# Channels 4 to 11 of a hybrid gMLP and attention step in pairs by seven half-length products, and gate sums in strips on the tensor engine

## The chip, the cores and the metric

The kernel runs on one core of a Trainium2 chip. The core has TensorE (PE in the profile, with its weight loads as PEld), VectorE (DVE), ScalarE (ACT), GpSimd (POOL) and SyncE (SP), which here issues the DMAs. Each engine has a queue of its own and works it off in order; engines wait for each other by semaphores. The metric is the device time of one execution in microseconds. Before the change the median of three runs is 626.75 us (626.26 to 626.86).

## The reference, cut to what matters

One step of a trunk with 128 context tokens and 1024 latent tokens, 1152 in all. The input is normalised, modulated and multiplied with one wide projection. Its columns are u, v and a gate g_a (512 each), the parts of the attention (c_q, c_kv, k_rope, together 448) and a gate g_b (512).

```python
def _front(x, cond, norm_g, w_ada, b_ada, w_in, w_s, b_s, g_v, q_norm_g, w_uq, kv_norm_g):
    mod = jax.nn.silu(cond) @ w_ada + b_ada
    shift, scale, gate = jnp.split(mod[:, None, :], 3, axis=-1)
    h = _rmsnorm(x, norm_g) * (1 + scale) + shift
    u, v, g_a, c_q, c_kv, k_rope, g_b = _split_in(h @ w_in)
    a_out = _chunk_mlp(u, v, w_s, b_s, g_v) * jax.nn.silu(g_a)
    ...

def _chunk_mlp(u, v, w_s, b_s, g_v):
    u = jax.nn.gelu(u)
    v = _rmsnorm(jax.nn.gelu(v).reshape(B, L, A_HEADS, A_HEAD_DIM), g_v)
    mixed = jnp.einsum('hpq,bnqhd->bnphd', w_s, v) + b_s.T[:, :, None]
    return u * mixed.reshape(B, L, A_WIDTH)

def _back(x, gate, a_out, attn, g_b, w_o):
    y = jnp.concatenate([a_out, attn * jax.nn.silu(g_b)], axis=-1) @ w_o
    return x + gate * y
```

## The kernel before

The transposed, modulated input h lies in SBUF as eight blocks of 128 features by three token groups of 384 tokens, each in two parts of a reduced format, a high part `hh[k, g]` and a low part `hl[k, g]` (the program's area0, area1 and area2 are the groups; a block's two parts stand side by side). A product of full precision takes three passes: high by high, high by low and low by high.

The twelve channel blocks of 128 columns are u (0 to 3, gelu), g_a (4 to 7, silu) and g_b (8 to 11, silu). For each block and group TensorE does 8 x 3 matmuls into one PSUM bank. For u and g_a, ScalarE writes the activation to SBUF and GpSimd multiplies it into `mixA`; for g_b ScalarE writes it into `mixB`. The weights of a channel come by one DMA of 512 KB (`w2r`) and are split into a high part (`w2h`, GpSimd) and a low part (`w2l`, VectorE).

The stages in order: modulation, transposes and the v projection; then a planned stretch (up to about 130 us) with the rest of v, channels 0 to 2 and the mixes `mixp` of the nine token tiles in four groups (0 to 2, 3 to 5, 6 and 7, 8); then channels 3 to 11 in a plain loop; then the z stage (`zacc`, from 245 us), attention and the output projection.

The planned stretch is written as steps with an engine, a cost, the steps they depend on and a priority. A planner replays them with these costs and records each engine's instructions in the order that comes out; this order is what the queues hold. The plain loop is recorded as it is written. There, beside the channels, `gate_sums` makes the third part of the modulation: VectorE multiplies each block of weights (`adag`) by a scalar per partition and adds it up (`matvec`, line 315), ScalarE and VectorE split the sums into two parts, and two matmuls with ones (line 830) add up the partitions. The weights of z (`wqr`, eight of 224 KB) are also split there, on GpSimd.

## Time and profile before

| What | Value |
|---|---|
| Median of three runs | 626.75 us |
| The profiled execution: its own time | 626.29 us |
| The profiled execution: span of its instructions | 624.5 us |
| GpSimd, ScalarE, VectorE busy | 29%, 42%, 58% of the span |
| Channels 3 to 11 on TensorE | 130.1 to 245.05 us |
| A w2r load of 512 KB, issue to landing, median | 3.9 us |

The span is what the trace covers; the rest of the execution's own time lies around it. Busy time of an engine is a sum over the whole span and says nothing of which engine is waited for; that is read from the chain of waits and from single stretches. Matmul records overlap, so their pace is the distance of their starts and not their duration.

### The profile page before, as it was taken

The page shows a single profiled execution, that of the slowest core. Times are in us where ns is not written, and L with a number is a line of the kernel's source. Part 1 is how long each engine was busy: PE and PEld are TensorE (multiplying, and loading weights), DVE is VectorE, ACT ScalarE, POOL GpSimd, SP SyncE. Part 2 cuts the span into 40 slices and gives each one's busy share as a digit, 9 for nine tenths or more (in the row PEclk, how much of TensorE's full clock was granted, in tenths as well). Part 3 has the DMA queues.
Part 4 walks back from the last instruction along what each step waited for, and adds up shares of the span by engine and source line. Part 5 has one row for each costly group of instructions (what it writes and reads, how often), then busy time and mean ns, then how long its engine had stood idle before and what let it go on. Part 6 is the DMA issues. An engine that isn't in the chain of part 4 may idle for free.

```text
span 624.5 us, 9810 instructions
## 1 busy us (share of the span) xinstructions
PE 610.4 (98%) x3703; PEld 555.3 (89%) x3703; DVE 364.4 (58%) x841; ACT 264.5 (42%) x636; POOL 178.8 (29%) x217
## 2 busy tenths in 40 slices
PE   7999999999999999999999999999999999999994
PEld 7678889999999999999997899999999988888884
DVE  4693466049556100476678657776666754587654
ACT  7556753112111111555676565555545632232212
POOL 2461223345545500443263212323222341000001
PEclk8999999999999999999999999999999999999998
DMA  8992000051331203000010000001101023423311
GB/s 319 391 373 69 1 34 2 2 180 71 116 108 58 94 8 110 27 2 1 1 41 1 2 0 2 1 2 35 35 1 34 35 69 129 142 101 135 128 41 68
DMA packets 15967, 46.32 MB, mean 74 GB/s; under 512 B 1952, under 2 KB 4912, under 8 KB 15920
## 3 DMA queue, kind: packets, MB, share of 16 engines
q1 hardware_dynamic: 15776, 45.51, 20.4%
q8 instruction: 29, 0.48, 0.3%
q10 hardware_dynamic: 144, 0.20, 0.1%
q14 instruction: 18, 0.15, 0.1%
...
## 4 chain that ended last, share of the span: by engine, by line
PE 92%; DVE 3%; ACT 2%; DMA 1%; issue 1%; SPq 0%; ACTq 0%; DVEq 0%
PE tp L746 6%; PE tp L159 6%; PE tp L157 6%; PE tp L158 6%; PE pT L1255 5%; PE w L1504 5%; PE w L1502 5%; PE w L1503 5%; PE o L1279 3%; PE o L1281 3%; PE o L1280 3%; PE s L1210 3%; PE s L1211 3%; PE s L1209 3%; PE s L1208 3%; PE s L1212 3%
## 5 line engine op out<-in xcount | busy, mean ns | idle before, releaser
L111 DVE TENSOR_TENSOR pl<-pT,ph 128x512 fp32r<-128x512 f32 x81 | 55.5, 687 | 48.4 <-ACT ph L1259 48.3
L1199 POOL TENSOR_SCALAR e<-e,rs 128x1280 f32<-128x1280 f32 x32 | 42.9, 1340 | 133.4 <-DVE rs L1198 121.1
L159 PE MATMUL tp<-area,w2l 128*128 128x384 f32 x216 | 72.5, 336 | 0.0
L157 PE MATMUL tp<-area,w2h 128*128 128x384 f32 x216 | 72.5, 336 | 0.0
L158 PE MATMUL tp<-area,w2h 128*128 128x384 f32 x216 | 72.5, 336 | 0.0
L1193 ACT ACTIVATE e<-s,nb,scl 128x256 f32<-128x256 f32 x64 | 56.1, 880 | 37.5 <-DVE nb L1187 37.5
L1259 ACT CAST ph<-pT 128x512 fp32r<-128x512 f32 x80 | 45.4, 588 | 42.0 <-PE pT L1255 39.0
L1255 PE MATMUL pT<-ident,e 128*128 128x128 f32 x320 | 48.0, 272 | 1.1 <-DVE pl L111 1.0
L1279 PE MATMUL o<-ph,vh 128*128 128x256 f32 x160 | 47.8, 299 | 0.0
L111 DVE TENSOR_TENSOR w2l<-w2r,w2h 128x1024 fp32r<-128x1024 f32 x12 | 19.9, 1655 | 45.7 <-POOL w2h L114 45.7
L1281 PE MATMUL o<-ph,vl 128*128 128x256 f32 x160 | 44.9, 281 | 0.0
L1280 PE MATMUL o<-pl,vh 128*128 128x256 f32 x160 | 44.7, 280 | 0.0
L1504 PE MATMUL w<-area,ml 128*128 128x512 f32 (+1 forms) x114 | 43.2, 379 | 0.0
L1255 PEld LDWEIGHTS pT<-ident,e 128*128 128x128 f32 x320 | 37.4, 140 | 4.6 <-issue 1.4
L157 PEld LDWEIGHTS tp<-area,w2h 128*128 128x128 f32 x216 | 40.5, 188 | 0.6 <-issue 0.5
L158 PEld LDWEIGHTS tp<-area,w2h 128*128 128x128 f32 x216 | 40.5, 188 | 0.2
L159 PEld LDWEIGHTS tp<-area,w2l 128*128 128x128 f32 x216 | 40.5, 188 | 0.0
L1208 PE MATMUL s<-kch,area 128*128 128x512 f32 (+2 forms) x100 | 39.2, 392 | 1.3 <-ACT e L1193 1.3
L1183 DVE TENSOR_REDUCE m<-s 128x1 f32<-128x1024 f32 x32 | 38.9, 1216 | 0.9 <-PE s L1212 0.8
L746 PE MATMUL tp<-area,w2h 128*128 128x384 f32 x144 | 37.3, 340 | 0.0
L1211 PE MATMUL s<-krh,area 128*128 128x512 f32 (+2 forms) x100 | 35.4, 354 | 0.0
L1210 PE MATMUL s<-kch,area 128*128 128x512 f32 (+2 forms) x100 | 35.4, 354 | 0.0
...
## 6 DMA issues: line engine op xcount, KB each, us to landing
...
```

The lines of the kernel that those rows point to most:

```text
L111: V.tensor_tensor(lo, src, f32(hi), op=ALU.subtract)
L157: T.matmul(ps, wh, xh, start=j == 0, stop=False)
L158: T.matmul(ps, wh, xl, start=False, stop=False)
L159: T.matmul(ps, wl, xh, start=False, stop=j == n - 1)
L746: T.matmul(tps[i, g][:, :GW], w_[i][:, k, :], x_[k, g], start=k == 0 and j == 0, stop=k == NK - 1 and j == 2)
L1193: S.activation(e[:, sl], src, AF.Exp, bias=nb, scale=scl[:, t : t + 1], accum_out=su[:, i : i + 1])
L1208: T.matmul(ps, qh_, kch[:, sl], start=True, stop=False)
L1255: T.transpose(ps[:, w : w + P], es[t, h][:, c * P : (c + 1) * P], ident)
L1279: T.matmul(o, vh[:, kt, :], ph[:, sl], start=c == 0, stop=False)
L1280: T.matmul(o, vh[:, kt, :], pl[:, sl], start=False, stop=False)
L1281: T.matmul(o, vl[:, kt, :], ph[:, sl], start=False, stop=c == n - 1)
L1504: T.matmul(ps, b, woh[k][:, c0:c1], start=False, stop=k == NK - 1)
```

## The change

Channels 0 to 3 are done as before, all in the planned stretch, which now goes on through all channels and the start of z. Channels 4 to 11 form four pairs (i, j). For token groups 0 and 1 the pair's 2 x 2 blocks (two channels by two halves of the features) times the input's 2 x 2 blocks (two halves by two groups) are done by seven products of half the length instead of eight, `p1` to `p7`: four use sums of input blocks (`t1` to `t4`), four use sums of weight blocks (`s1` to `s4`). The results are put together by additions from PSUM (`ka` to `kh`). Group 2 of these channels is done in the plain way.

The input sums are made once, by `input_sums`, on VectorE and GpSimd with ScalarE's casts; the first sum `t1` takes the place of `hh[k, 1]`, so `input_back` restores those blocks before z. The weight sums are made for each pair. High parts of weights from channel 2 on are made by ScalarE. The gate sums go to TensorE: eight matmuls into four strips of 32 partitions, then two matmuls with a selecting matrix; their load is one of 1 MB for each of four parts. The weights of z come in four loads, and their splits move to ScalarE, GpSimd and VectorE.

```diff
--- before.py
+++ after.py
@@ weights in parts @@
     def split_steps(i, deps):
         def hi():
-            a, b = ((0, 1), (2, 3), (6, 7))[i % 3]
-            w2hi[i] = slot(a, f"w2h{i}", [8, P], F32R)
-            w2lo[i] = slot(b, f"w2l{i}", [8, P], F32R)
-            pool_copy(w2hi[i], w2raw[i])
-        step(f"w2h{i}", "G", 1.01, hi, [f"w2r{i}", *deps], 2)
-        step(f"w2{i}", "V", 1.14, lambda: lo_of(w2lo[i], w2raw[i], w2hi[i]), [f"w2h{i}"], 3)
+            first = 6 if i == 2 else 8 if i == 3 else 2 * (i % 2)
+            w2hi[i], w2lo[i] = (weight_slot(first + m, f"w2{i}{m}", [8, P]) for m in range(2))
+            if i < 2:
+                pool_copy(w2hi[i], w2raw[i])
+            else:
+                S.copy(w2hi[i], w2raw[i])
+        step(f"w2h{i}", "G" if i < 2 else "S", 1.2, hi, [f"w2r{i}", *deps], 2)
+        step(f"w2{i}", "V", 1.4, lambda: lo_of(w2lo[i], w2raw[i], w2hi[i]), [f"w2h{i}"], 3)
@@ input sums, then undone @@
+    def input_sums(k, prio):
+        b11, b12, b21, b22 = ((f32(hh[kk, g]), f32(hl[kk, g])) for kk, g in ((k, 0), (k, 1), (k + 4, 0), (k + 4, 1)))
+        (h2, l2), (h3, l3) = T2[k], T3[k]
+        free = [f"v{t}" for t in range(5, 9)]
+        c = {}
+        ...
+        two("t1u", "G", made_in("u1", lambda: sub(G, c["u1"], b12[1], b11[1]), 2), ["sx", *older("t1s")])
+        two("t1a", "V", made_in("t1", lambda: sub(V, c["t1"], b12[0], b11[0])), ["sx"])
+        two("t1s", "V", lambda: add(V, c["t1"], c["t1"], c["u1"]), [f"t1u{k}", f"t1a{k}"])
+        two("t2a", "V", made_in("t2", lambda: sub(V, c["t2"], b22[0], c["t1"]), 2), [f"t1s{k}", *older("t2")])
+        two("t2s", "G", lambda: add(G, c["t2"], c["t2"], b22[1]), [f"t2a{k}"])
+        two("t2h", "S", lambda: S.copy(h2, c["t2"]), [f"t2s{k}", *free])
+        two("t3u", "G", made_in("u3", lambda: sub(G, c["u3"], b22[1], b12[1]), 3), [f"t3s{k - 1}"] if k else ["h27"], takes=("hf",))
+        two("t3a", "V", made_in("t3", lambda: sub(V, c["t3"], b22[0], b12[0]), 3), [f"t3u{k}"], takes=("hf",))
+        two("t3s", "V", lambda: add(V, c["t3"], c["t3"], c["u3"]), [f"t3a{k}"], gives=("hf",))
+        two("t3h", "S", lambda: S.copy(h3, c["t3"]), [f"t3s{k}", *free])
+        two("t3", "V", lambda: lo_of(l3, c["t3"], h3), [f"t3h{k}"], gives=("hf",))
+        two("t4a", "V", made_in("t4", lambda: sub(V, c["t4"], b21[0], c["t2"]), 2), [f"t2s{k}", *older("t4")])
+        two("t4s", "G", lambda: add(G, c["t4"], c["t4"], b21[1]), [f"t4a{k}"])
+        two("t4h", "S", lambda: (place(), S.copy(T4[k][0], c["t4"])), [f"t4s{k}", *free])
+        two("t4", "V", lambda: lo_of(T4[k][1], c["t4"], T4[k][0]), [f"t4h{k}"])
+        two("t2", "V", lambda: lo_of(l2, c["t2"], h2), [f"t2h{k}", f"t4a{k}"])
+        prio += 0.5
+        two("t1h", "S", lambda: S.copy(hh[k, 1], c["t1"]), [f"t1s{k}", f"t2a{k}", f"t3a{k}", *(f"tp{i}1" for i in range(4))])
+        two("t1", "V", lambda: lo_of(hl[k, 1], c["t1"], hh[k, 1]), [f"t1h{k}", f"t3u{k}"])
+    def input_back(k, prio, deps):
+        (a, b), (c, d) = (hh[k, 1], hl[k, 1]), (hh[k, 0], hl[k, 0])
+        f = {}
+        def begin(key, eng, x, y):
+            f[key] = pools["sx"].tile([P, 512], F32, tag=f"sf{key}", name=f"b{key}{k}")[:, :GW]
+            add(eng, f[key], f32(x), f32(y))
+        step(f"ba{k}", "G", 0.97, lambda: begin("a", G, a, c), [*deps, *([f"be{k - 1}"] if k else [])], prio, takes=("sfa",))
+        step(f"bb{k}", "V", 0.5, lambda: begin("b", V, b, d), [f"ba{k}"], prio, takes=("sfb",))
+        step(f"bc{k}", "V", 0.5, lambda: add(V, f["b"], f["b"], f["a"]), [f"bb{k}"], prio, gives=("sfa",))
+        step(f"bd{k}", "S", 0.48, lambda: S.copy(a, f["b"]), [f"bc{k}"], prio)
+        step(f"be{k}", "V", 0.5, lambda: lo_of(b, f["b"], a), [f"bd{k}"], prio, gives=("sfb",))
+    ...
@@ channel pairs @@
+    def pair_steps(n):
+        i, j = 4 + 2 * n, 5 + 2 * n
+        final = n == 3
+        before = [f"{p}_{n - 1}" for p in ("p5", "p6", "p7", "p3")] if n else ["tp22", "tp22", "tp32", "tp32"]
+        for c in (i, j):
+            deps = [f"w2{c - 2}"] if n == 0 else [f"s{m}a{n - 1}" for m in range(1, 5)] + [f"w2{c - 2}"]
+            load_step(f"w2r{c}", lambda c=c: load_w2(c), deps, 1.35)
+            split_steps(c, [f"tp{c % 2}2"] if n == 0 else [f"p{(2, 4)[c % 2]}_{n - 1}"])
+        ...
+        step(f"s1a{n}", "G", 1.28, block_sum(1, lambda: add(G, sf[1], blocks()[2], blocks()[3])), [*raws, "sx"], q, **own)
+        step(f"s2a{n}", "V", 0.68, block_sum(2, lambda: sub(V, sf[2], sf[1], blocks()[0])), [f"s1a{n}"], q, **two_)
+        step(f"s3a{n}", "G", 1.28, block_sum(3, lambda: sub(G, sf[3], blocks()[0], blocks()[2])), [f"s2a{n}"], q + 0.1, **own)
+        step(f"s4a{n}", "V", 0.68, block_sum(4, lambda: sub(V, sf[4], blocks()[1], sf[2])), [f"s3a{n}", f"s2{n}"], q, takes=("sfa",), gives=("sfb",))
+        for m, dep in ((1, [f"s2a{n}"]), (2, []), (3, []), (4, [])):
+            step(f"s{m}h{n}", "S", 0.6, lambda m=m: high(m), [f"s{m}a{n}", before[m - 1]], q + 0.15)
+            last = {} if m == 2 else dict(gives=("sfa",))
+            step(f"s{m}{n}", "V", 0.68, lambda m=m: lo_of(sw[m][:, 1, :], sf[m], sw[m][:, 0, :]), [f"s{m}h{n}", *dep], q + 0.15, **last)
+        ...
+        def product(key, w, x, deps):
+            def go(k0, k1):
+                if k0 == 0:
+                    banks[key] = bank(psa, "acc", f"{key}_{n}")[:, :GW]
+                passes = [(k, a_, b_) for k in range(k0, k1) for (wh, wl), (xh, xl) in ((w(k), x(k)),) for a_, b_ in ((wh, xh), (wh, xl), (wl, xh))]
+                for m, (k, a_, b_) in enumerate(passes):
+                    T.matmul(banks[key], a_, b_, start=k == 0 and m == 0, stop=k == 3 and m == len(passes) - 1)
+            in_turn(f"{key}_{n}a", 1.045, lambda: go(0, 2), deps, takes=("psa",))
+            in_turn(f"{key}_{n}", 1.045, lambda: go(2, 4), [])
+        ...
+        def seven():
+            t_ready = [[f"t{m}{k}" for k in range(4)] for m in range(1, 5)] if n == 0 else [[]] * 4
+            product("p1", weights(i, 0), inputs(0, 0), [f"w2{i}"])
+            product("p2", weights(i, 1), inputs(1, 0), [])
+            product("p6", weight_sum(2), lambda k: T2[k], [f"s2{n}", *t_ready[1]])
+            product("p7", weight_sum(3), lambda k: T3[k], [f"s3{n}", *t_ready[2]])
+            product("p4", weights(j, 1), lambda k: T4[k], [f"w2{j}", *t_ready[3]])
+            product("p5", weight_sum(1), lambda k: T1[k], [f"s1{n}", *t_ready[0]])
+            product("p3", weight_sum(4), inputs(1, 1), [f"s4{n}"])
+        if final:
+            seven()
+            plain()
+        else:
+            plain()
+            seven()
+        ...
+        def combine(key, out, key_ps, m, deps, **kw):
+            step(f"{key}{n}", "V", 0.55, lambda: add(V, out(), banks[key_ps], keep[m]), [f"{key_ps}_{n}", *(f"{d}{n}" for d in deps)], 0.5, gives=("psa",), **kw)
+        step(f"ka{n}", "S", 0.5, lambda: S.copy(kept("a"), banks["p1"]), [f"p1_{n}", "t33"], 0.5, takes=("ka",), gives=("psa",))
+        combine("kx", lambda: kept("x"), "p2", "a", ["ka"], takes=("tm",))
+        combine("kb", lambda: keep["a"], "p6", "a", ["kx"])
+        combine("kc", lambda: kept("c"), "p7", "a", ["kb"], takes=("kc",))
+        step(f"ke{n}", "V", 0.55, lambda: add(V, kept("d"), banks["p5"], keep["c"]), [f"p5_{n}", f"kc{n}"], 0.5, takes=("kd",))
+        combine("kg", lambda: keep["a"], "p5", "a", ["kc", "ke"])
+        step(f"kf{n}", "V", 0.55, lambda: add(V, keep["c"], banks["p4"], keep["c"]), [f"ke{n}", f"p4_{n}"], 0.5, gives=("psa",))
+        step(f"kh{n}", "V", 0.55, lambda: add(V, keep["a"], banks["p3"], keep["a"]), [f"kg{n}", f"p3_{n}"], 0.5, gives=("psa",))
+        for c, g, m, key, pool_ in ((i, 0, "x", "kx", "tm"), (j, 1, "d", "ke", "kd"), (j, 0, "c", "kf", "kc"), (i, 1, "a", "kh", "ka")):
+            gated(c, g, lambda m=m: keep[m], [f"{key}{n}"], (pool_,), lambda m=m: keep[m])
@@ gate sums @@
+    ...
+        def strips():
+            cell["ps"] = bank(pst, "t", f"gps{j}")
+            for kk in range(NK):
+                s_, i = kk % 4, kk // 4
+                T.matmul(cell["ps"][32 * s_ : 32 * s_ + 32, 0:256], csp[:, kk, :], cell["w"][:, kk, :], start=i == 0, stop=i == 1)
+        ...
+        load_step(f"ga{j}", fetch, ["vg", *([f"gr{j - 1}"] if j else [])], prio, cost=2.6)
+        step(f"gr{j}", "T", 0.7, strips, [f"ga{j}"], 4.0, takes=("pst",))
+        step(f"gh{j}", "S", 0.4, high, [f"gr{j}"], 1.0)
+        step(f"gl{j}", "V", 0.4, low, [f"gh{j}"], 1.0)
+        step(f"gt{j}", "T", 0.35, total, [f"gl{j}"], 4.0)
+        step(f"go{j}", "V", 0.35, out, [f"gt{j}"], 1.0, gives=("pst",))
@@ the plan @@
-        load_step("w2r2", lambda: load_w2(2), ["w20"], 1.35)
-        load_step("w2r3", lambda: load_w2(3), ["w21"], 2.5)
-        load_step("w2r4", lambda: load_w2(4), ["w22"], 2.5)
         ...
-        for n, (i, g) in enumerate(((0, 0), (1, 0), (0, 1), (1, 1), (2, 0), (2, 1))):
+        for n, (i, g) in enumerate(((0, 0), (1, 0), (0, 1), (1, 1))):
             channel_steps(i, g, 5 + 0.1 * n)
-        for i in range(3):
+        for i in range(2):
             channel_steps(i, 2, 6 + 0.1 * i, [f"h2{k}" for k in range(NK)])
-        split_steps(2, ["w2r2", "xT7"])
-        split_steps(3, ["tp02"])
-        split_steps(4, ["tp12"])
+        for n, (i, g) in enumerate(((2, 1), (3, 1), (2, 0), (3, 0), (2, 2), (3, 2))):
+            channel_steps(i, g, 6.2 + 0.01 * n)
+        for i in (2, 3):
+            load_step(f"w2r{i}", lambda i=i: load_w2(i), [f"w2{i - 2}"], 1.35)
+            split_steps(i, ["sx" if i % 2 else "xT7"])
+        all_channels()
         plan.run()
     ...
-    def gate_sums(j):
-        out = vg.tile([P, 2, 256], F32, tag="accg", name=f"accg{j}")
-        for hf_ in range(2):
-            ch = vg.tile([P, 4, 256], F32, tag="ada", name=f"adag{j}{hf_}", bufs=2)
-            nc.sync.dma_start(ch, I["ada_g"][j][:, 4 * hf_ : 4 * hf_ + 4, :])
-            for cond in range(2):
-                matvec(out[:, cond, :], [ch[:, i, :] for i in range(4)], cond, 4 * hf_)
-    ...
-    for i in range(3, 12):
-        if i + 2 < 12:
-            load_w2(i + 2)
-        gs = gate_sums(i - 4) if 4 <= i < 8 else None
-        for g in range(3):
-            channels(i, g)
-            if g == 0 and i + 2 < 12:
-                split_w2(i + 2)
-            if g == 0 and held is not None:
-                gate_row(i - 5, held)
-        held = gs
-        if i >= 4:
-            k = i - 4
-            raw = w1.tile([P, 512], F32, tag="wr", name=f"wqr{k}", bufs=2)
-            nc.sync.dma_start(raw[:, :448], I["w_q"][k])
-            wqh[k], wql[k] = split_w1(k, raw[:, :448], 448, "q")
-    closed(c_vg)
+    close_left("sx")
     closed(c_va)
```

The planner's order shows where work has moved. The first place is VectorE behind the last mix (`mixp8`) to the low half of channel 3's weights, before (`w2l3`):

```order
L691 SCALAR_TENSOR_TENSOR mixA_94<-mixp7_1166,cst_84,bsb_122 128x128 x4
L691 SCALAR_TENSOR_TENSOR mixA_94<-mixp8_1186,cst_84,bsb_122 128x128 x4
L111 TENSOR_TENSOR w2l3_1317<-w2r3_722,w2h3_1316 128x1024
L111 TENSOR_TENSOR w2l4_1367<-w2r4_919,w2h4_1366 128x1024
L111 TENSOR_TENSOR w2l5_1414<-w2r5_1383,w2h5_1413 128x1024
```

After, the low half is called `w231`; between the last mix and the first row shown here stand nine more operations of the same kinds (`t1f` to `t4f` are the sums of a block in full precision, `w1t` holds their parts):

```order
L808 TENSOR_TENSOR t1f3_1332<-area1_118,area0_117 128x384
L112 TENSOR_TENSOR w1t_120<-t2f0_1289,w1t_120 128x384
L808 TENSOR_TENSOR t4f1_1343<-area0_117,t2f1_1306 128x384
L808 TENSOR_TENSOR t2f2_1351<-area1_118,t1f2_1285 128x384
L112 TENSOR_TENSOR w1t_120<-t2f1_1306,w1t_120 128x384
L112 TENSOR_TENSOR w1t_120<-t4f0_1317,w1t_120 128x384
L805 TENSOR_TENSOR t1f3_1332<-t1f3_1332,u1f3_1308 128x384
L112 TENSOR_TENSOR w1t_120<-t4f1_1343,w1t_120 128x384
L808 TENSOR_TENSOR t4f2_1382<-area0_117,t2f2_1351 128x384
L808 TENSOR_TENSOR t2f3_1387<-area1_118,t1f3_1332 128x384
L112 TENSOR_TENSOR w1t_120<-t2f2_1351,w1t_120 128x384
L112 TENSOR_TENSOR w231_1265<-w2r3_716,w230_1264 128x1024
```

The low half has moved from directly behind the last mix to behind twenty operations of the input sums. On TensorE, from the last mix to the first matmul that reads channel 3's low half stand 146 matmuls before and 110 after. The second place is ScalarE at the start of the z stage, before:

```order
L801 ACTIVATE mixB_1379<-tp110_2265 128x384
L801 ACTIVATE mixB_1379<-tp111_2291 128x384
L801 ACTIVATE mixB_1379<-tp112_2317 128x384
L894 ACTIVATE wrh_2358<-rraw_2372,cst_84 128x256 x2
L959 COPY z0_2403<-zacc0_2378 128x448
```

And after:

```order
L890 ACTIVATE mixB_1871<-ka3_2274 128x384
L871 CAST area1_118<-bb0_2417 128x384
L890 ACTIVATE mixB_1871<-tp102_2385 128x384
L871 CAST area1_118<-bb1_2450 128x384
L890 ACTIVATE mixB_1871<-tp112_2421 128x384
L871 CAST area1_118<-bb2_2458 128x384
L871 CAST area1_118<-bb3_2465 128x384
L1398 ACT_TABLE_LOAD
L1398 ACTIVATE warm_e_2489<-ones_80 128x1
L1186 ACTIVATE wrh_2479<-rraw_2491,cst_84 128x256 x2
L1251 COPY z0_2522<-zacc0_2497 128x448
L1200 ACTIVATE j10_2525,ssz0_2523<-zacc0_2497 128x256
```

The casts of the restored blocks (`bb0` to `bb3`), a table load and the warm-up now stand ahead of the first copy of z; before, the table was loaded behind it.

239 lines of the change are left out of this document (187 added, 52 removed).

## The prediction

> **What bounds the kernel now.** I began with the page's totals and its chain of work, to see which engine sets the time.
>
> ```profile
> PE 610.4 (98%) x3703; PEld 555.3 (89%) x3703; DVE 364.4 (58%) x841; ACT 264.5 (42%) x636; POOL 178.8 (29%) x217
> PEclk8999999999999999999999999999999999999998
> PE 92%; DVE 3%; ACT 2%; DMA 1%; issue 1%; SPq 0%; ACTq 0%; DVEq 0%
> ```
>
> TensorE is busy in 610.4 of 624.5 us and carries 92% of the chain, at nearly full clock. An average over all stages doesn't say whether the changed stages are like that, so the busy time per stretch comes next (columns: length, busy time of each engine with its count of records, granted clock, DMA share, GB/s).
>
> ```profile
> 0.00:20.00 20.00, 16.61 (x115) 14.30 (x115) 9.80 (x28) 15.39 (x26) 4.72 (x10) 0.91 0.90 340
> 101.00:131.00 30.00, 30.00 (x180) 30.00 (x179) 6.54 (x18) 3.40 (x7) 9.77 (x10) 1.00 0.05 18
> 131.00:150.00 19.00, 19.00 (x109) 19.00 (x109) 14.42 (x20) 3.70 (x7) 9.75 (x9) 1.00 0.52 179
> 150.00:200.00 50.00, 50.00 (x287) 48.84 (x286) 32.63 (x61) 7.56 (x16) 23.72 (x19) 1.00 0.25 80
> 200.00:245.00 45.00, 45.00 (x261) 45.00 (x261) 3.53 (x4) 4.91 (x10) 11.45 (x12) 1.00 0.23 79
> ```
>
> From 101 to 245 us TensorE never stands, and VectorE and GpSimd are behind it with time to spare (6.5 and 9.8 of 30 us between 101 and 131). So here a matmul taken out is worth its whole pace, and any lateness that comes in is paid in full. Work taken off VectorE is worth nothing by itself.
>
> **What the change removes on TensorE.** The pace is read from the starts of single matmuls in the timeline, since the records overlap.
>
> ```profile
> 235.69 0.34 PE L157 MATMUL tp<-area,w2h 128*128 128x384 f32 x1
> 237.77 0.34 PE L157 MATMUL tp<-area,w2h 128*128 128x384 f32 x1
> 160.13 0.46 PE gps L830 x2
> 18.94 1.07 PE L326 MATMUL modp<-ada,csp 128*32 128x256 f32 x16
> ```
>
> Twelve matmuls lie between the first two rows: 2.08 / 12 = 0.173 us each. Before, the channels take 36 groups of 24, or 864. After, channels 0 to 3 keep 12 groups (288), eight plain groups remain for token group 2 (192), and four pairs take 7 products x 4 blocks x 3 passes (336): 816. That is 48 fewer, **-8.3 us**.
>
> The gate sums cost four times 0.47 = 1.9 us on TensorE. After, each has eight strip matmuls of the form of the last row (1.07 for 16, so 0.53 for 8) and two matmuls 256 wide, which I put at half of the 512-wide pair's 0.47, 0.24: 4 x 0.77 = 3.1 us, **+1.2**. Bounds for the pair are 0 and 0.47, or 4 x 0.24 either way. Without a wait anywhere, TensorE would be 7.1 us shorter, and VectorE loses the gate's multiply chain:
>
> ```profile
> L315 DVE SCALAR_TENSOR_TENSOR accg<-adag,csp,accg 128x256 f32<-128x256 f32 x56 | 28.3, 579 | 0.0
> ```
>
> These 28.3 us lay under matmuls, so they count for nothing.
>
> **What it adds, and beside what.** New are the input sums (40 VectorE operations 128x384, 16 on GpSimd, 16 ScalarE casts), the weight sums of each pair, seven PSUM additions per pair, and the sums undone at the end. Most have cover: a pair's VectorE work is 7 x 0.56 (additions), 6 x 0.69 (512-wide sums and low parts) and 2 x 1.21 (low halves) = 10.5 us, beside (84 + 48) x 0.173 = 22.8 us of matmuls. If that cover were gone the excess would stand in each of four pairs. What matters is where the order puts new VectorE work ahead of something TensorE will soon need, and what VectorE and GpSimd do to each other:
>
> ```profile
> 75.25 0.56 DVE L111 TENSOR_TENSOR area<-hf,area 128x384 fp32r<-128x384 f32 x1 [3.12 <-ACT hf L716]
> 64.85 0.69 DVE L682 TENSOR_TENSOR gv<-gv,vv3r 128x512 f32<-128x512 f32 x1
> 65.46 2.71 DVE L111 TENSOR_TENSOR area<-hf,area 128x384 fp32r<-128x384 f32 x2
> 159.69 1.21 DVE L111 TENSOR_TENSOR w2l<-w2r,w2h 128x1024 fp32r<-128x1024 f32 x1
> 123.65 2.04 DVE L111 TENSOR_TENSOR w2l<-w2r,w2h 128x1024 fp32r<-128x1024 f32 x1 [17.48 <-POOL w2h L114]
> 105.04 1.13 DVE L691 SCALAR_TENSOR_TENSOR mixA<-mixp,cst,bsb 128x128 f32<-128x128 f32 x4 [0.67 <-PE mixp L687]
> ```
>
> ```profile
> 64.97 2.79 POOL L682 TENSOR_TENSOR gv<-gv,vv3r 128x512 f32<-128x512 f32 x2 [16.27 <-DVE vv3r L131]
> 123.58 1.02 POOL L754 TENSOR_TENSOR mixA<-mixA,tmp 128x384 f32<-128x384 f32 x1
> 104.72 1.01 POOL L754 TENSOR_TENSOR mixA<-mixA,tmp 128x384 f32<-128x384 f32 x1 [0.81 <-ACT tmp L750]
> ```
>
> A 128x384 operation with both inputs in SBUF takes 0.56 us alone; two of them take 2.71 beside two GpSimd operations. The three VectorE rows from 64.85 run to 68.17, 3.3 us for 1.8 us of work: 0.75 lost per GpSimd operation. The low half takes 1.21 alone and 2.04 beside one: 0.83. Reads from PSUM (1.13 for four) are not stretched. I take 0.78 per GpSimd operation that meets dense VectorE work.
>
> *The low half of channel 3's weights.* Before, it stands right behind the last mix on VectorE, with 146 matmuls until TensorE uses it. After, twenty input-sum operations stand between, and 110 matmuls: 19.1 us of cover. VectorE needs 1.13 + 20 x 0.56 + 1.21 = 13.5 us alone; twelve GpSimd operations (eight sums, four gate products) fall into that stretch, 12 x 0.78 = 9.4, which makes 22.9, and 0.3 until the mix can be read. Hence a wait of 23.2 - 19.1 = **4.1 us** (0 if half of the contention shows, 6 if round trips between VectorE, GpSimd and ScalarE add 2). Behind TensorE's waiting matmul stand all later products; nothing can pass.
>
> *The first gate strips.* Their 1 MB load is issued only when VectorE has rewritten the third block of the first sum, some nine operations and two low halves later.
>
> ```profile
> 132.89 0.85 SPq L818 DMA_DIRECT2D adag<-in_ada_g  x2
> 138.36 0.62 DVE L313 TENSOR_SCALAR accg<-adag,csp 128x256 f32<-128x256 f32 x2 [2.95 <-DMA adag<-in_ada_g]
> ```
>
> The load takes 5.5 us from issue to use. VectorE reaches that point 9 us (alone) to 13 us (five GpSimd operations) after the low half, so data is there 37.7 to 42 us after the last mix; TensorE arrives after 204 matmuls and the wait above, 35.4 + 4.1 = 39.5. Between 0 and 2.5; I take **1.3**.
>
> *The second and third mix groups.* Here the third sums' operations enter between the mixes.
>
> ```profile
> 86.85 0.17 DVE L639 TENSOR_SCALAR vv3v<-ssv 128x12 f32<-128x12 f32 x1 [1.30 <-ACT junkv L673]
> 89.46 2.45 POOL L682 TENSOR_TENSOR gv<-gv,vv3r 128x512 f32<-128x512 f32 x2 [3.51 <-DVE vv3r L131]
> 91.04 1.95 PE L687 MATMUL mixp<-wsT,gv 128*128 128x128 f32 x16
> 98.67 2.04 POOL L682 TENSOR_TENSOR gv<-gv,vv2r 128x512 f32<-128x512 f32 x2 [6.76 <-DVE vv1t L129]
> 101.12 1.95 PE L687 MATMUL mixp<-wsT,gv 128*128 128x128 f32 x16
> ```
>
> For the second group VectorE gets four sums and channel 2's low half ahead (4 x 0.56 + 1.21 = 3.5, of which 1.3 fits the idle time of the first row) and GpSimd three operations (3 x 0.78 = 2.3): 4.5 us later, against 12 more matmuls ahead (2.1) and some 0.5 of slack (the first scaled tile is ready near 90.6). That leaves 1.9; as TensorE also has the earlier wait to itself I take **1.5** (0 to 3). For the third group 4 x 0.56 + 2 x 0.78 = 3.8 stands against 2.1 of matmuls and 1.4 of slack (99.7 to 101.1): 0.3; I take **0.5** (0 to 2).
>
> *The start of the z stage.* Undoing the sums is a chain of GpSimd, VectorE and ScalarE, whose last cast stands ahead of the table load, the warm-up and two weight parts, and all these ahead of the first z copy.
>
> ```profile
> 245.25 0.49 ACT L801 ACTIVATE mixB<-tp 128x384 f32<-128x384 f32 x1 [3.67 <-PE tp L159]
> 245.64 0.90 ACT L894 ACTIVATE wrh<-rraw,cst 128x256 fp32r<-128x256 f32 x2
> 250.21 0.53 ACT L959 COPY z<-zacc 128x448 f32<-128x448 f32 x1 [3.67 <-PE zacc L1097]
> 251.53 1.28 ACT L925 ACT_TABLE_LOAD   x1
> ```
>
> ```profile
> 250.79 0.20 PEld L972 LDWEIGHTS cqT<-ident,z 128*128 128x128 f32 x2 [0.39 <-ACT z L959]
> ```
>
> Measured from the end of the channels (245.05), the copy starts 5.2 us later. After, from the same point: the last channel's activation ends at 0.7, the third cast behind it at 1.2, its low part and two additions 1.7 plus hand-overs 0.4, last cast 3.8, table 5.1, warm-up 5.4, weight parts 6.3. So the copy is 1.1 late alone, of which nothing is left over for slack (TensorE already waited 0.39 for it before), and more with the GpSimd sums beside it: **+1.5** (0.5 to 2.5). The z stage's loads go out when the last pair's fifth product ends, 72 matmuls or 12.5 us ahead of it, against the 5.5 us above: hidden.
>
> The sum, against the profiled execution's 626.29: -8.3 + 1.2 + 4.1 + 1.3 + 1.5 + 0.5 + 1.5 = +1.8, **628.1 us**. That execution is 0.46 below the median of 626.75; 0.2% of the median (1.25 us), about what a measurement of this kernel can tell from no change, bounds "same" at 625.5 and 628.0.
>
> **The rivals.** *The cover holds.* If only every second GpSimd operation meets VectorE, the low half comes after 13.5 + 4.7 + 0.3 = 18.5 us, under 19.1, the strips' load lands in time, and mixes lose their 2.0. Left are -7.1 and 1.5: **620.7**. For it: GpSimd's own waits for ScalarE spread its work. Against: all rows above where both engines are dense show the full loss.
>
> *A long wait that also costs clock, slower than before.* If the sums' round trips lengthen VectorE's stretch by 2 us, TensorE stands 6 us in one piece. In the stretches above it stands only in the first, 3.4 of 20 us in several pieces, and there the granted clock is 0.91: 20 x 0.09 = 1.8 us lost, which I take as the price of a long stand. With 6.0, strips 2.5, mixes 2.0, z 2.0 and clock 1.8: 626.29 - 7.1 + 14.3 = **633.5**. It decides once the twenty operations take 22.5 us and not 20.6.
>
> The Trainium skill ("TensorE: Matmul & The Clock Gate", Part 1) says that an idle window of about 3.4 us halves the clock and that about 3.4 us of work restore it. The first stretch's 0.91 agrees in kind; no row here shows a gap that long in mid-kernel. By that rule the 4.1 us wait would add up to 1.7 us, giving 629.8; since the page calls the window free-running, a 4.1 us gap seldom holds a whole one.
>
> *The products don't flow.* If each pair's first product waits for weight sums by the length of one low half, 1.2 us, three pairs add 3.6 to the forecast: **631.7**. Against: the loads are issued when the previous pair's fourth sum is made, over 20 us ahead.
>
> **How the numbers follow.** Forecast 0.48 (its own terms spread it over 624.5 to 631), cover holds 0.27, long wait with clock 0.15, products don't flow 0.10. Faster: 0.27 and a fifth of the forecast's share, 0.09, together 0.36. Same: 0.21, the part of the forecast's share from 625.5 to 628.0. Slower: the remaining 0.18 of it and both slower rivals, 0.43. The range leaves out the lower part of "cover holds" and the upper part of the long wait, a tenth each: 620.3 to 633.5. The forecast's own range is 624.5 to 631.
>
> **What would show it.** In the profile after: TensorE's wait on channel 3's low half, near 4 us and ended by VectorE; twenty operations in some 20 us there; a wait ended by the gate's load; the first z copy 6 to 7 us after the last channel matmul. It is wrong if the dense operations stay near 0.6 us beside GpSimd, if TensorE waits in the pairs, or if 128x384 matmuls don't keep 0.173 us.

## The result, and the profile after

The changed kernel takes 636.46 us, the median of six executions (633.49 to 639.4), against 626.81 us (626.26 to 628.12) before on the same chip: a ratio of 1.015, with a 95% interval of 1.0121 to 1.0179. It is slower by 1.5%. The forecast was 628.1 us, its range ended at 633.5.

The profiled execution took 633.49 us over a span of 631.7, 7.20 more than the profiled one before. Four of the other five executions of the changed kernel ran at a lower mean granted clock (0.980 to 0.987, against 0.992 in the profile), so the median lies above the profile. In the execution that took 636.46 us, the clock was 0.987 over 634.7 us; that is 8.3 us at full loss, against 5.1 in the profile, about the 3.0 between them. One execution at 0.993 still took 635.79, so the clock is not the whole of the scatter.

The page's totals, clock and chain of the changed kernel:

```profile
PE 609.5 (96%) x3719; PEld 549.8 (87%) x3719; DVE 405.9 (64%) x886; ACT 293.9 (47%) x688; POOL 190.4 (30%) x223
PEclk9999998998999999999999999999999999999998
PE 80%; DVE 10%; DMA 4%; ACT 3%; issue 2%; POOL 1%; SPq 0%; DVEq 0%; ACTq 0%; POOLq 0%
```

TensorE's busy time fell by less than 1 us although 48 matmuls are gone, and its share of the chain fell from 92% to 80%: VectorE and the DMA now stand in the chain. The busy time per stretch says where:

```profile
85.00:101.00 16.00, 13.95 (x73) 12.66 (x72) 11.77 (x34) 6.52 (x30) 6.18 (x6) 0.89 0.11 34
101.00:131.00 30.00, 30.00 (x180) 30.00 (x180) 26.94 (x65) 9.50 (x24) 20.13 (x17) 1.00 0.00 1
131.00:150.00 19.00, 17.54 (x100) 17.22 (x99) 18.23 (x15) 7.13 (x14) 15.40 (x11) 1.00 0.10 28
150.00:200.00 50.00, 46.53 (x298) 41.95 (x297) 21.97 (x32) 15.80 (x27) 15.56 (x13) 0.97 0.38 127
200.00:245.00 45.00, 45.00 (x260) 45.00 (x259) 24.90 (x38) 16.56 (x29) 10.60 (x11) 1.00 0.19 65
```

Before, TensorE was busy without a break from 101 to 245 us. Now three stretches have a stand (TensorE idle), two of them at a lower clock, and VectorE is busy 26.9 of 30 us where it had 6.5. The last row shows that the pairs themselves flow. TensorE's timeline names the four stands that are new or longer:

```profile
94.84 2.97 PE L692 MATMUL mixp<-wsT,gv 128*128 128x128 f32 x16 [2.05 <-POOL gv L687]
...
133.56 1.68 PE L751 MATMUL tp<-area,w 128*128 128x384 f32 x8 [1.46 <-DVE w L112]
...
153.82 1.93 PE L1042 MATMUL gps<-adag,csp 128*32 128x256 f32 x16 [3.47 <-DMA adag<-in_ada_g]
...
258.40 0.44 PE L1264 MATMUL cqT<-ident,z 128*128 128x128 f32 x2 [1.49 <-ACT z L1251]
```

These are the second mix group, channel 3's low half, the first gate strips and the first z copy, the places that the prediction had named. What it had not put into its sum stands right behind two of them. Three-microsecond windows of the same trace (the granted clock is the third number from the end of a row):

```profile
93.00:96.00 3.00, 1.16 (x9) 1.16 (x10) 0.89 (x1) 0.00 (x0) 3.00 (x4) 0.96 0.00 0
96.00:99.00 3.00, 3.00 (x14) 3.00 (x14) 2.28 (x9) 2.74 (x13) 0.74 (x1) 0.50 0.03 8
99.00:102.00 3.00, 3.00 (x21) 3.00 (x20) 1.94 (x8) 2.37 (x13) 0.00 (x0) 0.97 0.00 0
...
153.00:156.00 3.00, 2.18 (x17) 0.91 (x18) 0.00 (x0) 0.18 (x1) 0.00 (x0) 0.63 0.06 25
156.00:159.00 3.00, 3.00 (x16) 2.88 (x16) 1.02 (x2) 0.38 (x2) 0.00 (x0) 0.80 0.62 213
```

In the first three windows 3 x (0.04 + 0.50 + 0.03) = 1.71 us of full clock are missing, in the last two 3 x (0.37 + 0.20) = 1.71 again. Each is a spell of 3.42 us at 0.50, and one such spell costs 1.71 us where TensorE is busy all through it.

From the first mix to the first z matmul is 171.6 us (79.7 to 251.3) after and 164.9 (80.2 to 245.1) before. Of the 171.6, 2.05 + 1.46 + 3.47 = 6.98 are stands, 3.42 is clock and 161.2 is the rest; before, all 164.9 is the rest. So without stands and clock the changed kernel gains 3.7 us there, and not the 7.1 that the prediction had.

### The profile page after: what moved, and what is told of

It is laid out like the page before. It is cut to its first block, busy times and chain, and to the rows that moved or that the text cites. A ratio compares the mean times of both kernels' runs of the same rounds, so it can differ in the third digit from the quotient of the medians.

```text
span 631.7 us, 9974 instructions
## 1 busy us (share of the span) xinstructions
PE 609.5 (96%) x3719; PEld 549.8 (87%) x3719; DVE 405.9 (64%) x886; ACT 293.9 (47%) x688; POOL 190.4 (30%) x223
## 3 DMA queue, kind: packets, MB, share of 16 engines
q1 hardware_dynamic: 15136, 45.50, 20.6%
## 4 chain that ended last, share of the span: by engine, by line
PE 80%; DVE 10%; DMA 4%; ACT 3%; issue 2%; POOL 1%; SPq 0%; DVEq 0%; ACTq 0%; POOLq 0%
PE p L956 9%; PE pT L1549 5%; PE w L1798 5%; PE w L1797 5%; PE w L1796 5%; PE tp L978 4%; PE o L1573 3%; PE o L1575 3%; PE o L1574 3%; PE s L1504 3%; PE s L1505 3%; PE s L1503 3%; PE s L1502 3%; PE s L1506 3%; PE tp L751 2%; PE zacc L1388 2%
## 5 line engine op out<-in xcount | busy, mean ns | idle before, releaser
L751 PE MATMUL tp<-area,w 128*128 128x384 f32 x288 | 53.8, 343 | 1.5 <-DVE w L112 1.5
L751 PEld LDWEIGHTS tp<-area,w 128*128 128x128 f32 x288 | 51.5, 191 | 2.2 <-DVE w L112 1.8
L978 PE MATMUL tp<-area,w 128*128 128x384 f32 x192 | 35.4, 342 | 0.0
L1503 PE MATMUL s<-kcl,area 128*128 128x512 f32 (+2 forms) x100 | 35.3, 353 | 0.0
L1506 PE MATMUL s<-krl,area 128*128 128x512 f32 (+2 forms) x100 | 35.1, 351 | 0.0
L978 PEld LDWEIGHTS tp<-area,w 128*128 128x128 f32 x192 | 34.3, 191 | 0.8 <-issue 0.8
L1897 POOL TENSOR_TENSOR z<-y,fg 128x256 f32<-128x256 f32 (+1 forms) x3 | 3.0, 998 | 95.8 <-DVE y L1892 95.8
L1573 PEld LDWEIGHTS o<-ph,vh 128*128 128x128 f32 x160 | 30.1, 188 | 1.6
```

Source lines behind the costliest of these rows:

```text
L751: T.matmul(tps[i, g][:, :GW], w_[i][:, k, :], x_[k, g], start=k == 0 and j == 0, stop=k == NK - 1 and j == 2)
L978: T.matmul(tps[c, 2][:, :GW], w_[c][:, k, :], x_[k, 2], start=k == 0 and m == 0, stop=k == NK - 1 and m == 2)
L1573: T.matmul(o, vh[:, kt, :], ph[:, sl], start=c == 0, stop=False)
```

## The experiments

Three theories. **A**: the loss is the stands at the named places plus the half clock behind them; taken away, the change is faster than before. **B**: the new work on VectorE and GpSimd is too much, and TensorE waits for it at one place if not at another. **C**: the lower clock is only what the profile records of a stand and costs nothing by itself. All times are medians; each ratio is to the kernel before on the same chip. The medians of the kernel before lie between 626.81 and 627.72 us on the chips used, so a difference between the medians of two runs is good to about 1 us; the stage from the first mix to z, read from the traces, is the finer measure, but of one execution each.

### Stands filled with work (e1_bridge)

```diff
+            for _ in range(10 if t == 3 else 0):
+                T.matmul(mps[t][:, :GW], hh[0, 0][:, :P], hh[0, 1], start=True, stop=True)
...
+            for _ in range(18 if j == 0 else 0):
+                T.matmul(cell["ps"][:, :GW], hh[0, 0][:, :P], hh[0, 2], start=True, stop=True)
```

The added products go into the second mix group's bank and the first gate's bank, which the real ones then overwrite.

> Eighteen matmuls without use stand ahead of the first gate strips and ten ahead of the fourth mix tile, in PSUM that the next matmuls overwrite, so that TensorE works (3.1 and 1.7 us) where it stood 3.5 and 2.05 us. Nothing is waited for less. Theory A (stands, and half clock for about 3.4 us behind each long one): both half-clock spells go, 1.7 us each, 636.5 becomes 633. Rival C (the granted clock is a record only; the stands alone cost): 636.5 within 0.5. Rival B (the new VectorE and GpSimd work is what TensorE waits for, wherever it waits): 636.5 as well.

Measured: 632.60 us, 1.0078 [1.0058, 1.0099], 3.9 us under the changed kernel. TensorE's timeline and a window of this kernel:

```profile
96.08 2.05 PE L694 MATMUL mixp<-wsT,gv 128*128 128x128 f32 x16 [0.34 <-POOL gv L687]
...
153.43 1.07 PE L1046 MATMUL gps<-adag,csp 128*32 128x256 f32 x16 [0.42 <-DMA adag<-in_ada_g]
```

```profile
90.00:105.00 15.00, 14.66 (x91) 14.03 (x90) 12.01 (x44) 7.11 (x31) 5.55 (x5) 1.00 0.10 35
```

Products that compute nothing (28 x 0.173 = 4.8 us) stand where TensorE stood; with the 2.2 us of stands left, that is 7.1, as much as the 6.98 before. All that has gone is the half clock, and 3.9 us with it by the medians; from the first mix to z are 168.5 us, 3.1 less than the 171.6, for two spells of 1.71. C falls: the spells cost their time.

### The gate's load issued earlier and its strips used later (e2_gate_late)

```diff
-        load_step(f"ga{j}", fetch, ["vg", *([f"gr{j - 1}"] if j else [])], prio, cost=2.6)
+        step(f"ga{j}", "D", 2.6, fetch, ["vg", *([f"gr{j - 1}"] if j else [])], prio, lag=7.0)
```

The strips now stand behind 240 matmuls from the last mix and not 204.

> The planner is told that a gate load lands 7 us after its issue instead of 2; the first strips then stand 36 matmuls (6.2 us) later on TensorE, nothing else is taken out. Theory A: the 3.5 us stand at the strips goes and the 1.7 us of half clock behind it, 636.5 becomes 631.3. Rival C: only the stand goes, 633.0. Rival B: the wait turns up in the pairs, 635 to 637.

Measured: 629.68 us, 1.0048 [1.0028, 1.0068]. The stand of 3.47 is gone. The second mix group still stands 2.06 us, but in this profile at full clock behind it (TensorE's row, then two windows):

```profile
95.40 2.05 PE L692 MATMUL mixp<-wsT,gv 128*128 128x128 f32 x16 [2.06 <-POOL gv L687]
```

```profile
93.00:96.00 3.00, 0.94 (x7) 0.62 (x7) 1.45 (x2) 0.00 (x0) 3.00 (x3) 1.00 0.00 0
96.00:99.00 3.00, 3.00 (x26) 3.00 (x25) 2.41 (x9) 2.32 (x10) 1.30 (x2) 1.00 0.03 8
```

The first mix to z takes 165.0 us, 6.6 less: 3.47 of stand and 3.42 of clock. Only one of the two spells is the edit's doing; that the 2.06 us brought none is this profile's luck, explained in the last section. As C has fallen, this is A. Little of the stand turned up elsewhere as B would have it: the first z copy stands 2.23 us where it stood 1.49.

### Channel 3's low half ahead of the input sums (e3_w3_first)

```diff
-        step(f"w2{i}", "V", 1.4, lambda: lo_of(w2lo[i], w2raw[i], w2hi[i]), [f"w2h{i}"], 3)
+        step(f"w2{i}", "V", 1.4, lambda: lo_of(w2lo[i], w2raw[i], w2hi[i]), [f"w2h{i}"], 1.5 if i == 3 else 3)
```

> The low half of channel 3's weights gets the priority to stand ahead of the input sums on VectorE. Theory A: the 1.5 us stand there goes, but the gate load's issue hangs on the same sums and TensorE is at the strips 1.5 us earlier, so that stand grows from 3.5 to about 5 us: 636.5 within 1. If the first stand were worth its time by itself: 635.0.

Measured: 632.38 us, 1.0078 [1.0056, 1.0101], better than expected by some 4 us. The wait on the low half is gone. TensorE then waits for the strips at an earlier time, for less than 3.47:

```profile
148.67 1.07 PE L1042 MATMUL gps<-adag,csp 128*32 128x256 f32 x16 [2.90 <-DMA adag<-in_ada_g]
```

No spell follows this stand (0.50 is nowhere between 147 and 153 us), one follows the mix group's and one the z copy's stand, 2.43 us here. So 2.90 us don't always bring a spell, and 2.06 sometimes do; the last section has the reason. Nor did the strips' wait grow to 5 us as expected. With the low half out of the way the gate's load is issued at 143.82, 5.3 us earlier than in the changed kernel (149.09), and the strips, which the planner now sets behind 186 matmuls from the last mix and not 204, wait less in spite of it.

### The third sums behind the last mix (e4_t3_late, e11_t3_mid)

In the changed kernel GpSimd waits for VectorE ahead of the scaled tile that the second mix group needs. GpSimd's timeline of the changed kernel:

```profile
92.23 1.24 POOL L808 TENSOR_TENSOR u3f<-area 128x384 f32<-128x384 f32 x1 [5.57 <-DVE w1t L112]
93.44 2.34 POOL L687 TENSOR_TENSOR gv<-gv,vv3r 128x512 f32<-128x512 f32 x2
```

The subtraction for the second `t3` waits for the low part of the first (their buffer), and `gv` is queued behind it. Two edits move the third sums, one behind all mixes, one behind the scaled tiles of the second group (block 1) or of the last (blocks 2 and 3):

```diff
-        two("t3u", "G", made_in("u3", lambda: sub(G, c["u3"], b22[1], b12[1]), 3), [f"t3s{k - 1}"] if k else ["h27"], takes=("hf",))
+        two("t3u", "G", made_in("u3", lambda: sub(G, c["u3"], b22[1], b12[1]), 3), [f"t3s{k - 1}"] if k else ["h27", "mix8"], takes=("hf",))
```

```diff
-        two("t3u", "G", made_in("u3", lambda: sub(G, c["u3"], b22[1], b12[1]), 3), [f"t3s{k - 1}"] if k else ["h27"], takes=("hf",))
+        two("t3u", "G", made_in("u3", lambda: sub(G, c["u3"], b22[1], b12[1]), 3), ([f"t3s{k - 1}", "gv5" if k == 1 else "gv8"]) if k else ["h27"], takes=("hf",))
```

> The third input sums may begin only behind the last mix. Theory A: the 2.05 us stand at the second mix group and the half clock behind it go, -3.7; VectorE has twelve more operations behind the last mix, which may cost up to 3 at the strips (TensorE gets there 30 matmuls later, 5.2 us, against 12 x 0.56 = 6.7): 633 to 635. Rival B: no gain, 636.5.

Measured: 638.41 us, 1.0167 [1.0143, 1.0191]; this expectation missed. The mix stands are gone, but thirty operations, ten more than in the changed kernel, now stand between the last mix and channel 3's low half on VectorE:

```profile
137.46 2.93 PE L751 MATMUL tp<-area,w 128*128 128x384 f32 x8 [7.13 <-DVE w L112]
```

```profile
138.00:141.00 3.00, 3.00 (x11) 3.00 (x10) 3.00 (x4) 0.51 (x1) 2.04 (x3) 0.50 0.55 175
141.00:144.00 3.00, 3.00 (x16) 3.00 (x15) 2.83 (x3) 1.96 (x3) 3.00 (x3) 0.81 0.00 0
```

The half clock lasts from 135.3 to 142.1 us here, two units of 3.42; its first 2.2 us lie within the stand and cost nothing.

> The kernel after with one edit: the third input sums of blocks 1 to 3 may begin on GpSimd only behind the scaled tiles of the second (block 1) and third mix group (blocks 2 and 3). If the 2.05 us stand at the second group comes from the order on GpSimd (a sum that waits for VectorE ahead of the scaled tile), it goes entirely and the half clock behind it (1.7) with it; six VectorE operations more then stand ahead of channel 3's low half (2.8 us, against 12 more matmuls, 2.1) and the strips come 12 matmuls later for them: 636.5 becomes 632 to 634. If it comes from VectorE's load before the mixes: 0.5 to 1 us of stand stay.

Measured: 632.54 us, 1.0095 [1.0073, 1.0117], 3.9 under the changed kernel. GpSimd and TensorE of this kernel:

```profile
90.88 2.77 POOL L687 TENSOR_TENSOR gv<-gv,vv3r 128x512 f32<-128x512 f32 x2 [4.07 <-DVE vv3r L132]
```

```profile
93.02 1.95 PE L692 MATMUL mixp<-wsT,gv 128*128 128x128 f32 x16
...
133.18 1.33 PE L751 MATMUL tp<-area,w 128*128 128x384 f32 x3 [3.54 <-DVE w L112]
```

The scaled tiles begin 2.6 us earlier and the second group stands no more, so the cause of the 2.05 is shown. The wait on the low half grew by the same 2.1 us to 3.54, that on the strips fell to 1.36: these two sum up to 4.90, as 1.46 and 3.47 did (4.93). Here they are one lateness of VectorE's stretch, and the first place where TensorE meets it takes what it can (in e3, where VectorE's order itself changed, the sum fell to 2.90). In place of two spells there is one. That much speaks for B: with the same work on VectorE, one stand alone can't be had away for nothing.

### All of them together, and what a matmul is worth (e5_all_fixed, e6_products_twice)

`e5` has the edits of e2, e3 and e11, and this one at the z stage:

```diff
-            S.activation(warm_e, ones[:, 0:1], AF.Sqrt)
```

`e6` is e5 with the first product of each pair computed twice, 48 matmuls more:

```diff
+                if key == "p1" and k0 == 0:
+                    for k in range(4):
+                        (wh, wl), (xh, xl) = w(k), x(k)
+                        for m, (a_, b_) in enumerate(((wh, xh), (wh, xl), (wl, xh))):
+                            T.matmul(banks[key], a_, b_, start=k == 0 and m == 0, stop=k == 3 and m == 2)
```

> Four edits of order together, no work taken out: the gate load told to land 7 us after issue; channel 3's low half ahead of the sums; the third input sums of blocks 1 to 3 behind the scaled tiles of the second and third mix group on GpSimd; the square-root table loaded after the first z copy, as before the change. Theory A: all four stands and the half clock behind them go, what is left is 48 matmuls saved (-8.3), the gates (+3.2 and about 1 for starting over beside them): 4 us under the kernel before, 623.5 (622 to 625). Rival B (the new work has to be waited for somewhere): 630 or more.

> e5 with the first product of each pair computed a second time, 48 matmuls 128x384 in all, as many as the seven products save. Theory A (a matmul taken out is worth its whole pace here): e5 plus 48 x 0.1735 = 8.3 us. If the saved matmuls had been hidden by other waits: less, down to 0.

Measured: e5 625.23 us, 0.997 [0.9959, 0.9981], and e6 633.71, 1.011 [1.0091, 1.0128]. Two stands are left in e5, 1.96 us on the strips (their place in the order had moved forward again) and 1.51 on the first z copy:

```profile
251.82 0.44 PE L1264 MATMUL cqT<-ident,z 128*128 128x128 f32 x2 [1.51 <-ACT z L1251]
```

Even so the change is faster than before; B in its strong form falls. The 48 matmuls cost 8.5 us by the medians and by the stage from the first mix to z (171.2 against 162.7): the -8.3 of the prediction holds. Without the strips' stand the stage would be 160.7 us, 4.1 less than before. So the other 4.2 of the 8.3 are neither in the matmuls nor in the stands.

### The early table alone (e12_no_early_table)

The last edit of e5 by itself.

> The kernel after without the warm-up that loads the square-root table ahead of the first z copy; the table is then loaded behind it, where it is first used, as in the kernel before. The 1.5 us stand at the first z tile shrinks to what the restored blocks' casts cost, 0.1 to 0.5: 635.4 from 636.5, a little more where that stand led to half clock.

Measured: 635.27 us, 1.0127 [1.0102, 1.0152], 1.2 under the changed kernel; the two intervals overlap, so the time alone shows no gain, and the rows decide. ScalarE's timeline, the changed kernel first:

```profile
255.63 1.28 ACT L1398 ACT_TABLE_LOAD   x1
...
257.04 0.89 ACT L1186 ACTIVATE wrh<-rraw,cst 128x256 fp32r<-128x256 f32 x2
257.83 0.51 ACT L1251 COPY z<-zacc 128x448 f32<-128x448 f32 x1
```

```profile
258.89 0.91 ACT L1186 ACTIVATE wrh<-rraw,cst 128x256 fp32r<-128x256 f32 x2
260.16 0.53 ACT L1251 COPY z<-zacc 128x448 f32<-128x448 f32 x1 [0.36 <-PE zacc L1389]
```

Without the table load ScalarE is early again and waits 0.36 for TensorE. The idle time of TensorE's weight loads ahead of the first z tile falls from 1.87 to 0.45 us, where it was 0.39 before the change; so in the changed kernel the table is what had made z late. It is not the only thing that can: e5 has no early table and still stands 1.51 us there, because the last cast of the restored blocks begins 5.4 us behind the first z matmul (250.02 against 244.67), and not 3.8 as in the changed kernel (255.10 against 251.27).

### Sums moved from GpSimd to VectorE (e7_sums_on_vector, e8_all_fixed_vector)

```diff
-        two("t1u", "G", made_in("u1", lambda: sub(G, c["u1"], b12[1], b11[1]), 2), ["sx", *older("t1s")])
+        two("t1u", "V", made_in("u1", lambda: sub(V, c["u1"], b12[1], b11[1]), 2), ["sx", *older("t1s")])
...
-        two("t2s", "G", lambda: add(G, c["t2"], c["t2"], b22[1]), [f"t2a{k}"])
+        two("t2s", "V", lambda: add(V, c["t2"], c["t2"], b22[1]), [f"t2a{k}"])
...
-        two("t4s", "G", lambda: add(G, c["t4"], c["t4"], b21[1]), [f"t4a{k}"])
+        two("t4s", "V", lambda: add(V, c["t4"], c["t4"], b21[1]), [f"t4a{k}"])
```

`e7` is the changed kernel with this, `e8` is e5 with it.

> The kernel after with twelve of the sixteen GpSimd sums moved to VectorE, the rest as it was. Between the last mix and channel 3's low half stand then 35 sums on VectorE instead of 20, and TensorE has 126 matmuls (21.9 us) of cover. If the two engines slow each other: 35 x 0.47 + five GpSimd products x 0.82 = 20.6 us, where 20 sums took 17.7 beside twelve: the stand is 0 to 2 us. If VectorE simply takes 0.89 us for such a sum: 31 us, a stand of 10.

> e5 with the same twelve sums on VectorE. Theory A: e5 has no stand in this stretch any more, so within 1 us of e5.

Measured: e7 635.94 us, 1.0144 [1.0125, 1.0164], not clear of the changed kernel's 1.015. Why this helps little and misses its expectation, VectorE's and GpSimd's timelines of e7 show:

```profile
126.39 0.55 DVE L805 TENSOR_TENSOR t1f<-t1f,u1f 128x384 f32<-128x384 f32 x1
126.86 0.55 DVE L808 TENSOR_TENSOR t1f<-area,area 128x384 f32<-128x384 f32 x1
...
131.87 1.09 DVE L112 TENSOR_TENSOR w1t<-t2f,w1t 128x384 fp32r<-128x384 f32 x1 [1.19 <-ACT w1t L844]
...
135.05 1.05 DVE L112 TENSOR_TENSOR t4l<-t4f,w1t 128x384 fp32r<-128x384 f32 x1 [1.62 <-ACT w1t L852]
```

```profile
114.55 6.92 POOL L759 TENSOR_TENSOR mixA<-mixA,tmp 128x384 f32<-128x384 f32 x2 [3.24 <-ACT tmp L755]
```

The sums do run at their own pace, one every 0.47 us. But VectorE now comes to the low parts before ScalarE has cast them, and waits 1.55, 1.19 and 1.62 us for casts that are queued behind activations; TensorE's stand on channel 3's low half is 3.85. Fewer contended operations alone are no remedy where the order makes VectorE wait.

In e8 the low half is early, and but for 0.54 us at the first z copy nothing stands. It takes **622.42 us, 0.9936 [0.9914, 0.9959]**, less than both kernels. It is 2.8 us under e5, where within 1 was expected: the expectation had overlooked e5's two stands. Its total and the first gate on TensorE's timeline:

```profile
PE 605.5 (98%) x3719; PEld 546.9 (88%) x3719; DVE 405.0 (65%) x898; ACT 293.3 (47%) x687; POOL 177.3 (29%) x211
```

```profile
144.67 6.45 PE L978 MATMUL tp<-area,w 128*128 128x384 f32 x36
151.05 1.07 PE L1042 MATMUL gps<-adag,csp 128*32 128x256 f32 x16
152.05 2.36 PE L956 MATMUL p<-area,w 128*128 128x384 f32 x12
154.25 0.28 PE L1054 MATMUL gps<-hig,selr 128*2 128x256 f32 x1
154.37 0.28 PE L1054 MATMUL gps<-log,selr 128*2 128x256 f32 x1
154.48 2.29 PE L956 MATMUL p<-area,w 128*128 128x384 f32 x12
156.61 4.37 PE L956 MATMUL p<-w1t,s 128*128 128x384 f32 x24
```

VectorE has as much work as in the changed kernel (405.0 against 405.9 us), so it was never too much, only in the wrong order. From the first mix to z are 160.7 us, without a stand or a spell: 4.2 less than before. The rows say where the other 4.1 of the 8.3 are: eight strips take 1.00 us (151.05 to 152.05), the pair of sums 0.23; ahead of the strips 36 x 0.173 = 6.2 leaves 0.15 of 6.38, behind them twelve take 2.20 in place of 2.08, behind the pair 2.13. That is about 1.5 for each gate, against 0.47 before.

### The strips themselves (e10_half_strips, e9_gates_on_vector)

`e10` is e8 with four strip matmuls per gate in place of eight; half of the gate's sum is left out.

```diff
-            for kk in range(NK):
-                s_, i = kk % 4, kk // 4
-                T.matmul(cell["ps"][32 * s_ : 32 * s_ + 32, 0:256], csp[:, kk, :], cell["w"][:, kk, :], start=i == 0, stop=i == 1)
+            for s_ in range(4):
+                T.matmul(cell["ps"][32 * s_ : 32 * s_ + 32, 0:256], csp[:, s_, :], cell["w"][:, s_, :], start=True, stop=True)
```

> e8 with four strip matmuls for each gate and not eight (half of the gate's sum is left out). If eight cost 1.0 us, as the trace has it: -2.0, 620.4. If they cost the 0.53 of my prediction: -1.1, 621.3.

Measured: 621.89 us, 0.9905 [0.9883, 0.9927]; from the first mix to z 159.3 us, 1.4 less than e8, between the two expectations. (By the medians it is 0.5 less, but its four executions ran at a lower clock, 0.990 to 0.993 against 0.992 to 0.998, so the stage is the better measure.) Its strips:

```profile
152.77 0.64 PE L1041 MATMUL gps<-adag,csp 128*32 128x256 f32 x8
153.34 2.35 PE L956 MATMUL p<-area,w 128*128 128x384 f32 x12
```

Four matmuls leave eight records and take 0.57 us (152.77 to 153.34). So a strip matmul of these 32-bit inputs counts two records, and the row of 16 was eight matmuls: 1.0 us for a gate, not 0.53.

`e9` is e8 with the gate sums back on VectorE, in pieces between its other work:

```diff
-        step(f"gr{j}", "T", 0.7, strips, [f"ga{j}"], 4.0, takes=("pst",))
...
+        PR = 0.4
...
+        for q, (cond, half) in enumerate(((0, 0), (0, 1), (1, 0), (1, 1), (0, 2), (0, 3), (1, 2), (1, 3))):
+            step(f"gm{j}{cond}{half}", "V", 0.98, lambda cond=cond, half=half: sums(cond, half), [last, f"ga{j}" if half < 2 else f"gb{j}", *([f"gl{j - 1}"] if j else [])], PR)
```

> e8 with the gate sums back on VectorE, as in the kernel before (multiply chains, then two matmuls with ones), planned among the pairs in pieces of two operations. On TensorE a gate then costs 0.47 us again and not about 1.3 with what it starts over: -3.3, 619.1 from 622.4. VectorE has 28 us more of work under the pairs' 115 us; if that comes between a product and its addition, TensorE waits for banks and the gain is less or turns round.

Measured: 633.27 us, 1.0093 [1.0075, 1.0111], a miss. VectorE takes the pieces ahead of weight sums and low halves, and channel 8's low half comes late. VectorE's row and then TensorE's:

```profile
207.00 1.22 DVE L112 TENSOR_TENSOR w<-w2r,w 128x1024 fp32r<-128x1024 f32 x1
```

```profile
208.28 5.54 PE L978 MATMUL tp<-area,w 128*128 128x384 f32 x22 [8.78 <-DVE w L112]
```

The price of the strips itself comes out as expected: from the first mix to z TensorE is busy for 159.04 us, 3.15 of them at half clock, which is 157.5 at full clock against e8's 160.7, 3.2 less for the four gates. The stands, 12.35 us in all in that stage, take it back and more. So whether the sums on VectorE with a better place would beat the strips stays open; the run shows only that this place is worse.

## Why the prediction was wrong

| Term | Forecast, us | In the changed kernel, us |
|---|---|---|
| 48 matmuls | -8.3 | -8.3 (e6: 8.5 for 48) |
| Gate sums on TensorE | +1.2 | +4.6 (+4.1 in e8) |
| Channel 3's low half | +4.1 | 1.46 |
| First gate strips | +1.3 | 3.47 |
| Second and third mix group | +1.5 and +0.5 | 2.05 and 0 |
| Start of z | +1.5 | 1.87 - 0.39 = 1.5 |
| Half clock behind stands | 0 | 3.42, more in the median |
| The rest (first mix 0.5 earlier, behind the channels 0.5 less) | 0 | -1.0 |
| Sum | +1.8 | +7.2 |

**The step that failed is the sum's last one: it priced every wait at its own length, with nothing for the clock behind it. A second term of the same size, the gate sums, was mis-sized.** The profile is 5.4 us above the forecast: 3.4 are the half clock, 3.4 the gates, the rest takes 1.4 back. All four places were right, and together they are 8.5 us where the prediction had 8.9. The clock behind them was put into one rival alone, at one stand of 6 us. In fact 2.05 us were enough, and the bound from the kernel's start (1.8 us for 0.91 over 20) was one such spell, 12.5 to 15.9 us in that trace. That rival's 633.5 is the profiled execution's time by luck: its stand of 6 us is not there, two spells are in place of one, and the gates make up the rest.

The Trainium skill ("TensorE: Matmul & The Clock Gate", Part 1) gives a window of about 3.4 us that halves the clock, and the spells of 3.42 us at 0.50 agree with its length. The prediction read from it that a 4.1 us gap seldom holds a whole idle window. The runs differ: stands of 2.05 us brought a spell, so no whole window need be idle, and by the windows read in the last section a gap of 4.1 us has at least half of it, 2.05, in one of them wherever it lies.

**The gate sums were mis-sized by a count.** The working took 16 records in the modulation's row for 16 matmuls and halved its 1.07. They were eight. With the pair's 0.24 (0.12 apart in two rows of e8) that makes 4 x 1.24 - 1.9 = +3.1 in place of +1.2, and gaps of about 0.3 in all around each gate bring it to the +4.1 that e8 shows. (The changed kernel's own stage leaves +4.6, of which 0.5 is not explained. Its first mix comes 0.5 us earlier than before as the profile before has a spell at its start, 12.5 to 15.9 us, and this one none.)

**The low half** came sooner than forecast. VectorE's timeline of the changed kernel:

```profile
115.15 0.55 DVE L808 TENSOR_TENSOR t1f<-area,area 128x384 f32<-128x384 f32 x1
...
117.54 1.35 DVE L805 TENSOR_TENSOR t1f<-t1f,u1f 128x384 f32<-128x384 f32 x1 [0.91 <-POOL u1f L808]
118.81 1.37 DVE L808 TENSOR_TENSOR t2f<-area,t1f 128x384 f32<-128x384 f32 x1
...
131.48 2.02 DVE L112 TENSOR_TENSOR w<-w2r,w 128x1024 fp32r<-128x1024 f32 x1
```

The twenty operations take from 113.74 to 131.48, 17.7 us for a forecast 20.6. Their pace alone is 0.47 (the start of the next), not the record's 0.56, and nine, not twelve, are contended, at 1.29 each: 11 x 0.47 + 9 x 1.29 + 0.91 = 17.7. The price of contention, 1.29 - 0.47 = 0.82, is close to the forecast's 0.78; the number of operations that met it lies between the forecast's twelve and the six of "the cover holds".

**The strips** waited longer because TensorE waited less at the low half: in e11 and the changed kernel both waits together are 4.9 us, against 5.4 in the forecast. The load's row says the same; it was issued at 149.09 and landed for TensorE at 153.8, 41.4 us behind the last mix (forecast 37.7 to 42):

```profile
149.09 0.33 SPq L1034 DMA_DIRECT2D adag<-in_ada_g  x1
```

**The mixes** had the right sum (2.0 against 2.05) by luck, from another cause: not VectorE's length but GpSimd's wait ahead of the scaled tile, shown by e11. **The z start** was right in mechanism and size (e12; the last cast was put at 3.8 us and began at 3.83). **The products flow**, as the forecast had it: no stand between 200 and 245 us.
